# A causal mask inside the scan, a convolution summed in PSUM, and value transposes through the dense products' banks: a hybrid decoder block on one core

## The chip, the core and the metric

The kernel runs on one core of one Trainium2 chip. A core has TensorE (PE in the profile, with its weight loads as PEld), VectorE (DVE), ScalarE (ACT), GpSimd (POOL), and SyncE (SP), which here issues most transfers. Matmuls write to the eight banks of PSUM; DVE and ACT read and write those banks and the on-chip memory SBUF; POOL in this kernel works on SBUF alone.

The metric is the device time in microseconds of one execution. One more execution was recorded by the hardware profiler, and what is said about engines comes from that one.

## The reference

One layer on 1024 tokens with 16 learned tokens in front (1040 positions) and 1024 features. Two branches read the same normalised input: a gated short convolution and stick-breaking attention with 16 heads of 64.

```python
h = xn @ w_in
b_c, c_c, h_c, q, k, v, g_conv, g_attn = jnp.split(h, list(splits), axis=-1)
y_conv = b_c * causal_dwconv(c_c * h_c, conv_w_mix)
branch_conv = y_conv @ w_proj_conv
...
z = jnp.einsum("bqhd,bkhd->bhqk", qb, kb, ...) * scale
causal = s_idx < t_idx
log_beta = jax.nn.log_sigmoid(z)
log_fail = jnp.where(causal, log_beta - z, 0.0)
survive = lax.cumsum(log_fail, axis=3, reverse=True) - log_fail
a = jnp.where(causal, jnp.exp(log_beta + survive), 0.0)
o = jnp.einsum("bhqk,bkhd->bqhd", a, vb)
...
merged = gate_conv * branch_conv + gate_attn * branch_attn
return merged @ w_out
```

The weight of key s for query t is sigmoid(z) times the product, over the keys between s and t, of sigmoid(-z). Keys at or after t have weight 0, and their factor in the product is 1. The convolution has width 3 along positions, one set of three weights for each channel. A gated MLP with a second such convolution follows. All inputs are float32.

## The kernel before, in words

**Exact products from rounded parts.** Every operand of a large product is split into a rounded part and a remainder (`split`, lines 63 to 65: a cast on ACT, a subtraction on DVE or POOL), and a product takes three matmuls: hi x hi, hi x lo, lo x hi (lines 124 to 126).

**The dense products.** `Dense` walks a list of items. An item is 128 output features: 128 columns of a weight matrix, three chunks of about 342 positions, eight steps of three matmuls for a chunk. Before an item starts, the next item's weights are split: ACT writes `whi` (line 64), then POOL writes `wlo` (line 65). A chunk's result is taken from its bank by the item's `evac`. The banks come from `ps_mm`, three of them in turn. `dense.defer(n, fn)` runs `fn` when n further steps have been written.

**Attention.** It works by pairs of heads (8 pairs), and a head in 3 groups of 3 blocks of 114 queries. `stage1` computes for each block the scores z in up to three pieces (lines 325, 326; two banks, `ps_z`), and ACT makes `fl` = sigmoid(-z) and `be` = sigmoid(z). Then `weights`, one step late, does the following: DVE sets the factors on and above the diagonal to 1 by a maximum with the constant `ones_up` over the last 114 columns (line 335), then runs a product scan from the right over all nk columns (line 336, `fl` both as the factor and as the second operand of a minimum); POOL multiplies the scan into `be` (line 338) and zeroes the upper triangle (line 339). The nine widths nk are 128, 242, ... 1040. `stage2` transposes `be` on TensorE into two banks in turn (`ps_tp`, line 372), ACT and DVE split it to `ah` and `al`, and TensorE multiplies with the values (lines 362, 363). A third transpose needs the bank of the first, so it waits until DVE has written that `al`.

**Order.** The program is written as one stream. The loop after line 480 takes steps of `stage1` and `stage2` in turn, by a table of costs, and spends on every step a share of dense steps, so that a pair's own 21 or so dense chunks are done when its attention is done. Each engine executes its own instructions strictly in the order in which the build has placed them. The items of a pair are: three for the convolution (c, h, b), a gate, then value, query and key of the next pair.

**The three places that change.** The convolution: after the third chunk of item h, `conv3` makes `yy` of all 1026 positions at once, a scaled copy on ACT (line 196) and two multiply-adds on DVE (lines 197, 198). The values: `item_v` collects `vt`, and in the three following steps `tokens` transposes it, nine blocks of 128 positions, into the same two `ps_tp` banks (line 257), with a split to `vv` on ACT and DVE. The end of a group: ACT copies one half of `av` to `otmp`, and DVE adds the other half into `ot` (lines 389, 390).

## Time and profile before

| | us |
|---|---|
| three timed runs | 2075.9, 2072.39, 2073.58 |
| median | 2073.58 |
| profiled execution | 2082.49 |
| its span, first to last instruction | 2080.6 |

The median is the time to compare with. Sums made from the profile refer to 2082.49 us and its span; the profiled execution is 8.9 us above the median.

The page gives each engine's busy time, groups of equal instructions, and waits. A matmul's record overlaps the next one's, so TensorE's rate is read from the distance between starts, or from a count in a stretch. In a timeline row the columns are the start in us from the span's start, the duration in us, the engine, the line, the operation with output and inputs, the shapes, and in brackets the idle time before it and what ended it. In the table by stretches the last three columns are the granted clock of TensorE, the busy share of the DMA engines and GB/s.

The span falls into a start (to about 60 us), the attention stage with its dense products (60 to about 1060), the rest of the mixer (to about 1400) and the MLP.

### The profile page before, as it was taken

How to read it: one execution, taken by the hardware profiler on the slowest of the kernel's cores; microseconds unless marked ns; L12 is line 12 of the kernel's file. 1: busy time of each engine (PE TensorE's matmuls, PEld its weight loads, DVE VectorE, ACT ScalarE, POOL GpSimd, SP SyncE). 2: the span in 40 equal slices, each digit the busy share in tenths (PEclk: the TensorE clock that was granted, in tenths of full speed). 3: DMA queues.
4: the chain of work that ended last, by engine and by line, in shares of the span. 5: the costliest groups of instructions: out<-in, count | busy, mean ns of one | idle time of the engine just before them, and what ended most of it. 6: DMA issues, size and time to landing. Idle time of an engine off the chain costs nothing.

```text
span 2080.6 us, 30846 instructions
## 1 busy us (share of the span) xinstructions
PE 1990.9 (96%) x12228; PEld 1861.3 (89%) x12228; DVE 1076.3 (52%) x1689; ACT 851.0 (41%) x1771; POOL 900.2 (43%) x764
## 2 busy tenths in 40 slices
PE   5999999999999999999999989979999999999997
PEld 4999998998999999999999989978898899878886
DVE  6455565655556565654342114785444444445546
ACT  4444454545445454544441213354334434412122
POOL 4343443434344434434212551225655555555353
PEclk9999999999999999999999999989999999999999
DMA  3111101111111101111375674313222122253323
GB/s 134 41 51 41 61 32 51 42 41 52 41 51 42 61 31 52 41 41 61 124 241 173 170 197 132 104 52 102 77 86 82 62 101 66 77 182 102 101 81 132
DMA packets 56029, 177.57 MB, mean 85 GB/s; under 512 B 12728, under 2 KB 12728, under 8 KB 55884
## 3 DMA queue, kind: packets, MB, share of 16 engines
q1 hardware_dynamic: 52560, 165.09, 24.5%
q10 hardware_dynamic: 3324, 10.50, 1.6%
q8 instruction: 96, 1.57, 0.3%
q14 instruction: 49, 0.40, 0.1%
HBM read 131.36 MB, written 44.21 MB: 84 GB/s over the span
## 4 chain that ended last, share of the span: by engine, by line
PE 80%; DVE 9%; ACT 3%; DMA 3%; POOL 2%; issue 2%; DVEq 0%; ACTq 0%; SPq 0%; POOLq 0%
PE mm L124 13%; PE mm L125 12%; PE mm L126 12%; PE st L861 6%; PE st L865 6%; PE st L863 6%; PE st L1155 3%; PE st L1153 3%; PE st L1154 3%; PE tp L372 3%; PE av L362 2%; PE av L363 2%; PE z L326 2%; PE z L325 2%; DVE fl L336 2%
## 5 line engine op out<-in xcount | busy, mean ns | idle before, releaser
L124 PE MATMUL mm<-xnT,whi 128*128 128x342 f32 (+2 forms) x1536 | 506.6, 330 | 3.6 <-ACT xnT L64 3.6
L125 PE MATMUL mm<-xnT,whi 128*128 128x342 f32 (+2 forms) x1536 | 495.4, 323 | 0.5 <-DVE xnT L65 0.5
L126 PE MATMUL mm<-xnT,wlo 128*128 128x342 f32 (+2 forms) x1536 | 492.2, 320 | 0.0
L338 POOL TENSOR_TENSOR be<-be,fl 114x127 f32<-114x127 f32 (+2 forms) x144 | 177.1, 1230 | 412.0 <-DVE fl L336 187.0
L124 PEld LDWEIGHTS mm<-xnT,whi 128*128 128x128 f32 x1536 | 291.0, 190 | 8.4 <-ACT xnT L64 4.1
L125 PEld LDWEIGHTS mm<-xnT,whi 128*128 128x128 f32 x1536 | 291.7, 190 | 2.2 <-DVE xnT L65 1.0
L126 PEld LDWEIGHTS mm<-xnT,wlo 128*128 128x128 f32 x1536 | 290.9, 189 | 0.0
L65 POOL TENSOR_TENSOR wlo<-raw,whi 128x1024 fp32r<-128x1024 f32 x80 | 201.6, 2520 | 187.2 <-ACT whi L64 175.6
L65 POOL TENSOR_TENSOR a_op<-raw,a_op 128x512 fp32r<-128x512 f32 (+1 forms) x136 | 192.2, 1426 | 89.4 <-ACT a_op L64 86.7
L336 DVE TENSOR_TENSOR_SCAN fl<-fl 114x128 f32<-114x128 f32 (+2 forms) x144 | 209.0, 1451 | 4.9
L65 DVE TENSOR_TENSOR al<-tp,ah 128x342 fp32r<-128x342 f32 (+4 forms) x288 | 127.0, 450 | 139.7 <-ACT ah L64 137.6
L64 ACT CAST ah<-tp 128x342 fp32r<-128x342 f32 (+4 forms) x288 | 113.1, 398 | 194.2 <-PE tp L372 185.8
L861 PE MATMUL st<-opT,a_op 128*128 128x258 f32 (+2 forms) x528 | 171.9, 325 | 4.7 <-ACT snap L876 1.7
L863 PE MATMUL st<-opT,a_op 128*128 128x258 f32 (+2 forms) x528 | 169.8, 322 | 2.9 <-DVE opT L65 2.0
L865 PE MATMUL st<-opT,a_op 128*128 128x258 f32 (+2 forms) x528 | 169.3, 321 | 0.0
L327 ACT ACTIVATE fl<-z 114x348 f32<-114x348 f32 (+10 forms) x240 | 111.5, 465 | 131.9 <-PE z L326 124.5
L64 ACT CAST a_op<-raw 128x512 fp32r<-128x512 f32 (+1 forms) x136 | 85.0, 634 | 156.2 <-DMA raw<-in_w_up_gate_dram 51.2
L372 PE MATMUL tp<-ident,be 114*128 114x114 f32 x720 | 119.7, 263 | 29.5 <-DVE al L65 25.1
L1160 DVE TENSOR_TENSOR acc<-acc,st 128x512 f32<-128x512 f32 x144 | 98.5, 687 | 91.2 <-PE st L1155 91.2
L372 PEld LDWEIGHTS tp<-ident,be 114*128 114x128 f32 x720 | 89.0, 138 | 44.6 <-DVE al L65 34.3
L863 PE MATMUL st<-opB,a_op 128*128 128x512 f32 (+2 forms) x396 | 127.4, 322 | 0.0
L861 PE MATMUL st<-opB,a_op 128*128 128x512 f32 (+2 forms) x396 | 127.3, 321 | 0.0
(172 smaller groups left out, 4408.8 us busy)
## 6 DMA issues: line engine op xcount, KB each, us to landing
raw<-in_w_in_dram SPq DMA_DIRECT2D x64, 512.0 KB
raw<-in_w_up_gate_dram SPq DMA_DIRECT2D x44, 512.0 KB
act_d<-owork SPq DMA_DIRECT2D x22, 512.0 KB
araw<-act_d SPq DMA_DIRECT2D x22, 512.0 KB
raw<-in_w_down_dram SPq DMA_DIRECT2D x22, 512.0 KB
y_d<-yy SPq DMA_DIRECT2D x8, 513.0 KB
ga_d<-gt SPq DMA_DIRECT2D x8, 513.0 KB
o_d<-ot SPq DMA_DIRECT2D x8, 513.0 KB
```

The lines of the kernel that those rows point to most:

```text
L64: nc.scalar.copy(hi, src)
L65: (lo_engine or nc.vector).tensor_tensor(lo, src, hi.bitcast(F32), op=ALU.subtract)
L124: nc.tensor.matmul(ps, wh, xh, start=(kb == 0), stop=False)
L125: nc.tensor.matmul(ps, wh, xl, start=False, stop=False)
L126: nc.tensor.matmul(ps, wl, xh, start=False, stop=(kb == KB - 1))
L327: nc.scalar.activation(fl[:, c0:c0 + n], z, AF.Sigmoid, scale=-0.125)
L336: nc.vector.tensor_tensor_scan(fl[:, :nk][:, ::-1], fl[:, :nk][:, ::-1], fl[:, :nk][:, ::-1], 1.0, op0=ALU.mult, op1=ALU.min)
L338: nc.gpsimd.tensor_tensor(be[:, 0:nk - 1], be[:, 0:nk - 1], fl[:, 1:nk], op=ALU.mult)
L372: nc.tensor.transpose(tp[:n, QB * j:QB * (j + 1)], blocks[j][0][:, kb * P:kb * P + n], ident[:QB, :QB])
L861: nc.tensor.matmul(ps, wt[:, 0, k], xh, start=start and kb == 0, stop=False, skip_group_check=True)
L863: nc.tensor.matmul(ps, wt[:, 0, k], xl, start=False, stop=False, skip_group_check=True)
L865: nc.tensor.matmul(ps, wt[:, 1, k], xh, start=False, stop=stop and kb == 3, skip_group_check=True)
```

## The change

- **Mask.** `ones_up` (114 x 114) becomes `upper` (114 x 1040), zero but for the last 114 columns, which hold the triangle of ones. The maximum on DVE ahead of the scan is gone. The scan multiplies as before, and its second operation is now a maximum with `upper` instead of a minimum with `fl`: 1 on and above the diagonal, at least 0 elsewhere.
- **Convolution.** It is done after each chunk of item h instead of after the third, 342 positions at a time. The scaled copy goes to a bank of `ps_mm` (`yacc`), the first multiply-add works in that bank, the second writes `yy` in SBUF. Two DVE instructions of 1026 become six of 342; one on ACT becomes three.
- **Values.** The transposes go to banks of `ps_mm` (`vtp`), and at steps 4, 12 and 20 after the value item instead of 1, 2 and 3. `ps_tp` is left to the attention weights.
- **End of a group.** ACT copies into `ot` itself; `otmp` is gone.
- **Constants.** The table of channel constants is loaded in two parts: 40 columns at the start, 66 later, behind `early`. The start-up pool has two buffers for each tag instead of four.

```diff
-    par = const.tile([P, 106], F32, name="par")
+    par = const.tile([P, 40], F32, name="par")
...
-    ones_up = xnt_pool.tile([QB, QB], F32, name="ones_up")
-    nc.gpsimd.memset(ones_up, 0.0)
-    nc.gpsimd.affine_select(out=ones_up, in_=ones_up, pattern=[[-1, QB]], compare_op=ALU.is_gt,
-                            fill=1.0, base=0, channel_multiplier=1)
+    upper = xnt_pool.tile([QB, NT], F32, name="upper")
+    nc.gpsimd.memset(upper, 0.0)
+    nc.gpsimd.affine_select(out=upper[:, NT - QB:], in_=upper[:, NT - QB:], pattern=[[-1, QB]],
+                            compare_op=ALU.is_gt, fill=1.0, base=0, channel_multiplier=1)
...
-                tp = ps_tp.tile([P, 512], F32, name="tp", tag="tp")
+                tp = ps_mm.tile([P, 512], F32, name="vtp", tag="mm")
...
-            dense.defer(1, lambda: tokens(0, 4, P))
-            dense.defer(2, lambda: tokens(4, 4, P))
-            dense.defer(3, lambda: tokens(8, 1, 16))
+            dense.defer(4, lambda: tokens(0, 4, P))
+            dense.defer(12, lambda: tokens(4, 4, P))
+            dense.defer(20, lambda: tokens(8, 1, 16))
...
             nc.vector.tensor_tensor(c, c, ps, op=ALU.mult)
-            if ci == 2:
+            if ci == 0:
                 st["y"] = work.tile([P, NT], F32, name="yy", tag="wk", bufs=4)
-                conv3(st["y"][:, :NQ], st["c"], NQ, lambda k: w_mix(k, cb))
+            j = ci * CH
+            y, src = st["y"][:, j:j + CH], st["c"][:, j:]
+            acc = ps_mm.tile([P, 512], F32, name="yacc", tag="mm")[:, :CH]
+            nc.scalar.activation(acc, src[:, 2:2 + CH], AF.Copy, scale=w_mix(2, cb))
+            nc.vector.scalar_tensor_tensor(acc, src[:, 1:1 + CH], w_mix(1, cb), acc,
+                                           op0=ALU.mult, op1=ALU.add)
+            nc.vector.scalar_tensor_tensor(y, src[:, 0:CH], w_mix(0, cb), acc,
+                                           op0=ALU.mult, op1=ALU.add)
...
-                nc.vector.tensor_tensor(fl[:, nk - QB:nk], fl[:, nk - QB:nk], ones_up, op=ALU.max)
                 nc.vector.tensor_tensor_scan(fl[:, :nk][:, ::-1], fl[:, :nk][:, ::-1],
-                                             fl[:, :nk][:, ::-1], 1.0, op0=ALU.mult, op1=ALU.min)
+                                             upper[:, NT - nk:][:, ::-1], 1.0,
+                                             op0=ALU.mult, op1=ALU.max)
...
-        tmp = work.tile([P, CH], F32, name="otmp", tag="otmp")
         a, b = (0, 64) if h == 0 else (64, 0)
-        nc.scalar.copy(tmp[a:a + 64], av[b:b + 64])
-        nc.vector.tensor_tensor(ot[a:a + 64, CH * g:CH * (g + 1)], av[a:a + 64], tmp[a:a + 64],
-                                op=ALU.add)
+        o = ot[a:a + 64, CH * g:CH * (g + 1)]
+        nc.scalar.copy(o, av[b:b + 64])
+        nc.vector.tensor_tensor(o, av[a:a + 64], o, op=ALU.add)
...
+    par_ffn = early.tile([P, 66], F32, name="par_ffn")
+    nc.sync.dma_start(par_ffn, channels[:, 40:])
```

The build places each engine's instructions anew. Two places on DVE are shown, first before and then changed. `cc` is the convolution's input, `fl` the factors of the scan, `al` the split of the transposed weights, for which TensorE waits.

DVE at the third chunk of item h, before: the chunk's product, both multiply-adds with a split between them, the splits, and later the mask and scan of 698 columns.

```order
L276 TENSOR_TENSOR cc<-cc,mm 128x342
L197 SCALAR_TENSOR_TENSOR yy<-cc,par,yy 128x1026
L65 TENSOR_TENSOR al<-tp,ah 128x342
L198 SCALAR_TENSOR_TENSOR yy<-cc,par,yy 128x1026
L65 TENSOR_TENSOR al<-tp,ah 128x228
L65 TENSOR_TENSOR al<-tp,ah 100x114
L283 TENSOR_TENSOR yy<-yy,mm 128x342
L335 TENSOR_TENSOR fl<-fl,ones_up 114x114
L336 SCALAR_TENSOR_TENSOR fl<-fl 114x698
```

DVE at the same place, changed (the listing names the scan like a multiply-add; it is the row that writes `fl`):

```order
L343 SCALAR_TENSOR_TENSOR fl<-fl,upper 114x584
L277 TENSOR_TENSOR cc<-cc,mm 128x342
L284 SCALAR_TENSOR_TENSOR yacc<-cc,par,yacc 128x342
L343 SCALAR_TENSOR_TENSOR fl<-fl,upper 114x698
L286 SCALAR_TENSOR_TENSOR yy<-cc,par,yacc 128x342
L65 TENSOR_TENSOR al<-tp,ah 128x228
L65 TENSOR_TENSOR al<-tp,ah 100x114
```

The scan of 698 columns has moved from behind the two splits to ahead of them, between the chunk's two multiply-adds.

ACT at the same place, changed: the cast of the next weights and then the scaled copy.

```order
L336 ACTIVATE be<-z 114x350
L64 CAST whi<-raw 128x1024
L283 ACTIVATE yacc<-cc,par 128x342
L335 ACTIVATE fl<-z 114x348
L336 ACTIVATE be<-z 114x348
```

The scaled copy stands behind the cast of the weights, as the copy of 1026 did.

DVE where the values are split, before:

```order
L65 TENSOR_TENSOR vv<-tp,vv 128x8x64
L335 TENSOR_TENSOR fl<-fl,ones_up 114x114
L336 SCALAR_TENSOR_TENSOR fl<-fl 114x584
L65 TENSOR_TENSOR vv<-tp,vv 128x8x64
L65 TENSOR_TENSOR vv<-tp,vv 16x2x64
L335 TENSOR_TENSOR fl<-fl,ones_up 114x114
L336 SCALAR_TENSOR_TENSOR fl<-fl 114x698
L65 TENSOR_TENSOR al<-tp,ah 128x342
```

And changed:

```order
L343 SCALAR_TENSOR_TENSOR fl<-fl,upper 114x470
L343 SCALAR_TENSOR_TENSOR fl<-fl,upper 114x584
L65 TENSOR_TENSOR vv<-vtp,vv 128x8x64
L343 SCALAR_TENSOR_TENSOR fl<-fl,upper 114x698
L65 TENSOR_TENSOR al<-tp,ah 128x342
```

One split of values instead of three stands ahead of the weights' split; the other two follow later, among the query's.

More of the change, by code (lines that the diff above doesn't have):

```diff
@@ L192, in w_ffn @@
     def w_ffn(k, b):
-        return par[:, 40 + k * NFF + b:40 + k * NFF + b + 1]
+        return par_ffn[:, k * NFF + b:k * NFF + b + 1]
     def conv3(dst, src, n, wt):
@@ L429, in block_kernel @@
     with ExitStack() as p0:
-        small = p0.enter_context(pool("p0s", 4, "right"))
+        small = p0.enter_context(pool("p0s", 2, "right"))
         gb = work.tile([P, NT], F32, name="gb", tag="wk", bufs=4)[:, :D]
         junk = work.tile([P, NT], F32, name="junk", tag="wk", bufs=4)[:, :D]
-        warm = small.tile([P, 1], F32, name="warm", bufs=1)
+        warm = small.tile([P, 1], F32, name="warm", tag="v")
         nc.vector.memset(warm, 1.0)
@@ L470, in block_kernel @@
         dense.load(1)
-        nc.sync.dma_start(par, channels)
+        nc.sync.dma_start(par, channels[:, :40])
         start_items(x_block)
```

## The prediction

> **What bounds the kernel.** I read the table by stretches first: the two halves of the attention stage (60 to 1060 us, where nearly every edited line works) and a stretch of dense products alone. Each row gives PE, PEld, DVE, ACT, POOL busy with counts, then granted clock, DMA share, GB/s.
>
> ```profile
> 110.00:600.00 490.00, 472.94 (x3062) 454.43 (x3061) 285.04 (x440) 237.36 (x545) 200.07 (x224) 0.99 0.14 47
> 600.00:1060.00 460.00, 447.89 (x2915) 432.60 (x2915) 248.81 (x395) 227.46 (x518) 182.62 (x193) 1.00 0.20 64
> 1060.00:1150.00 90.00, 90.00 (x577) 90.00 (x576) 25.77 (x46) 18.78 (x34) 19.21 (x8) 1.00 0.61 195
> ```
>
> TensorE bounds it: 577 matmuls in 90 us are 0.156 us each at full rate, and in the attention stage TensorE lacks only 17.1 + 12.1 = 29 us of work in 950. DVE, which the change relieves, is little over half busy there, so DVE time is worth something only where TensorE waits for it. The waits of PE say where (us, times, longest):
>
> ```profile
> PE tp L372 <- DVE al L65: 25.1, 20, 2.6
> PE tp L372 <- DVE vv L65: 4.4, 6, 0.7
> ```
>
> So 29.5 us, all transposes of weights held by a DVE split. That is the ceiling of the direct gain. The timeline shows them at four kinds of place; in each I ask what the changed order puts ahead of the split.
>
> **Place 1: the mixer convolution, once in each of 8 pairs.** Start, duration, instruction; brackets give the idle time before.
>
> ```profile
> 329.93 1.38 DVE L336 TENSOR_TENSOR_SCAN fl<-fl 114x584 f32<-114x584 f32 x1
> 331.30 0.51 DVE L276 TENSOR_TENSOR cc<-cc,mm 128x342 f32<-128x342 f32 x1
> 333.28 3.21 DVE L197 SCALAR_TENSOR_TENSOR yy<-cc,par,yy 128x1026 f32<-128x1026 f32 x1 [1.47 <-ACT yy L196]
> 336.41 0.50 DVE L65 TENSOR_TENSOR al<-tp,ah 128x342 fp32r<-128x342 f32 x1
> 331.14 1.06 ACT L64 CAST whi<-raw 128x1024 fp32r<-128x1024 f32 x1
> 332.09 1.15 ACT L196 ACTIVATE yy<-cc,par 128x1026 f32<-128x1026 f32 x1
> 331.45 1.23 POOL L338 TENSOR_TENSOR be<-be,fl 114x583 f32<-114x583 f32 x1 [1.38 <-DVE fl L336]
> 333.01 2.39 POOL L65 TENSOR_TENSOR wlo<-raw,whi 128x1024 fp32r<-128x1024 f32 x1
> 336.96 0.30 PE L372 MATMUL tp<-ident,be 114*100 114x114 f32 x1 [1.57 <-DVE al L65]
> L283 DVE TENSOR_TENSOR yy<-yy,mm x24: 478/490/512, 111.1 to 935.0; 128x342 f32<-128x342 f32 x24
> ```
>
> L197 reads two SBUF operands. It starts 0.27 us behind POOL's `wlo` and ends 1.09 us after it (336.49 against 335.40): DVE stood until POOL had finished. L283 has one operand in PSUM, and its 24 calls spread only from 478 to 512 ns. So the new additions, with the running sum in PSUM, should not be held: I take 0.45 us for one (a third of 1.27 us, the free width-1026 call, is 0.42; L283 has 0.49), and 0.5 us for the ACT product (bounds 0.38, a third of L196, and 1.15).
>
> The Trainium skill (SBUF — State Buffer, "Who interferes with whom") states just that: an instruction of DVE with two SBUF inputs and one of GpSimd that reads SBUF exclude each other whole, and one SBUF input leaves DVE free. Trace and rule agree at L197 and L283, and the rule also speaks against the change: the new scan still has two SBUF inputs.
>
> That is where the stall goes. In the new order the 698-wide scan comes third, between the two additions of the last chunk, ahead of the splits. When does it start? The ACT product stands behind the weight cast (ends 332.20), so 332.2 + 0.5 + 0.45 plus handshakes is 333.2; and 0.4 us of transposes now stand ahead of the chunk's last matmul, which moves the cast too: 333.6. `wlo` follows the 584-wide scan (end 331.31) by 1.70 us, and that scan moves by under 0.1: 333.1. POOL wins by 0.5 us. The scan then runs from about 335.2 (as L197 did) for 1.65, the second addition to 337.35, the split of 228 to 337.7. PE resumes at 337.7, not 336.96, with 0.4 us more work behind it (two weight-value products, a transpose and a score product more, a dense matmul less). Net **+0.3 us** a pair, times 8 = **+2.4**. If the scan wins instead, the split ends at 336.0: -1.35 a pair, -10.8. Upper bound: a further 0.7 us for slow PSUM additions, +8.
>
> **Place 2: values, 6 pairs.** The nine value transposes held the two `tp` banks, and the splits `vv` stood in DVE's queue.
>
> ```profile
> 388.50 1.15 DVE L335 TENSOR_TENSOR fl<-fl,ones_up 114x114 f32<-114x114 f32 x1
> 389.69 1.38 DVE L336 TENSOR_TENSOR_SCAN fl<-fl 114x584 f32<-114x584 f32 x1
> 392.59 1.65 DVE L336 TENSOR_TENSOR_SCAN fl<-fl 114x698 f32<-114x698 f32 x1
> 394.16 0.78 DVE L65 TENSOR_TENSOR al<-tp,ah 128x342 fp32r<-128x342 f32 x2
> 387.13 2.39 POOL L65 TENSOR_TENSOR wlo<-raw,whi 128x1024 fp32r<-128x1024 f32 x1
> 391.21 1.22 POOL L338 TENSOR_TENSOR be<-be,fl 114x583 f32<-114x583 f32 x1 [1.69 <-DVE fl L336]
> 391.70 0.51 PE L372 MATMUL tp<-ident,be 114*128 114x114 f32 x3 [0.74 <-DVE vv L65]
> 394.70 0.30 PE L372 MATMUL tp<-ident,be 114*100 114x114 f32 x1 [0.86 <-DVE al L65]
> ```
>
> The first idle time (0.74) goes: the values have other banks. The second is a chain. Without its mask the 584-wide scan waits for the same `wlo` (to 389.52) and ends at 390.7, not 391.06. One `vv` split still stands behind it (0.55, to 391.25), so POOL's `be` product, 0.15 us after the scan's end as before (391.06 to 391.21), is first again and holds the 698-wide scan until about 392.0. Scan to 393.6, split to 394.0, PE resumes at 394.05. That is 0.65 earlier, but five of the nine value transposes (0.1 us each, the last short: 0.45) are still to do: **-0.2** a pair, **-1.2**. Bounds: both idle times gone, -1.6 a pair, -10; above, 0.4 us at the first key chunk, which now waits for a query chunk emptied eight steps earlier, +3.
>
> **Place 3: the longest scan against `wlo`.** The same contest, lost and won:
>
> ```profile
> 352.06 0.37 DVE L335 TENSOR_TENSOR fl<-fl,ones_up 114x114 f32<-114x114 f32 x1 [1.62 <-ACT fl L327]
> 352.46 4.40 DVE L336 TENSOR_TENSOR_SCAN fl<-fl 114x1040 f32<-114x1040 f32 x1
> 352.27 2.41 POOL L65 TENSOR_TENSOR wlo<-raw,whi 128x1024 fp32r<-128x1024 f32 x1
> 357.32 0.52 PE L372 MATMUL tp<-ident,be 114*128 114x114 f32 x3 [1.95 <-DVE al L65]
> 589.90 2.33 DVE L336 TENSOR_TENSOR_SCAN fl<-fl 114x1040 f32<-114x1040 f32 x1
> 589.98 4.43 POOL L65 TENSOR_TENSOR wlo<-raw,whi 128x1024 fp32r<-128x1024 f32 x1
> 472.01 4.39 DVE fl L336
> ```
>
> At 352 POOL was 0.19 us ahead and the scan took 4.40; at 590 DVE was 0.08 ahead and `wlo` took 4.43, which cost PE nothing. Without the mask the scan starts where the mask did, 0.3 to 0.4 us earlier, and wins. The loss occurs in two pairs (the last row, from the chain of waits, is the other): 2 x 2.1 = **-4.2** (bounds -4.2 and 0).
>
> **Place 4: the last pair.**
>
> ```profile
> 972.48 1.38 DVE L336 TENSOR_TENSOR_SCAN fl<-fl 114x584 f32<-114x584 f32 x1
> 974.06 2.62 DVE L336 TENSOR_TENSOR_SCAN fl<-fl 114x698 f32<-114x698 f32 x1
> 974.00 1.22 POOL L338 TENSOR_TENSOR be<-be,fl 114x583 f32<-114x583 f32 x1 [1.69 <-ACT ah L64]
> 977.14 0.43 PE L372 MATMUL tp<-ident,be 114*100 114x114 f32 x1 [2.58 <-DVE al L65]
> ```
>
> Here no `vv` stands between the scans; without the mask the second follows at once and beats `be`. The first starts 0.3 earlier, the second ends at 975.1 and not 976.7: **-1.6**.
>
> **The clock.** A wait costs more than its length where it empties a slot of 3.41 us:
>
> ```profile
> 335.28:338.69 3.41, 1.83 (x12) 1.47 (x12) 3.41 (x6) 0.26 (x1) 0.23 (x2) 1.00 0.46 154
> 338.69:342.11 3.42, 3.42 (x14) 3.38 (x14) 2.52 (x4) 1.35 (x3) 1.12 (x1) 0.50 0.00 0
> 219.22:222.63 3.41, 1.82 (x12) 1.29 (x10) 3.41 (x5) 0.26 (x1) 0.47 (x2) 1.00 0.48 154
> 222.63:226.04 3.41, 3.41 (x23) 3.38 (x23) 2.76 (x5) 1.64 (x4) 0.87 (x1) 1.00 0.02 5
> 458.16:461.57 3.41, 3.41 (x13) 3.37 (x14) 2.61 (x4) 1.35 (x3) 1.02 (x1) 0.50 0.00 0
> 976.98:980.40 3.42, 3.26 (x13) 3.26 (x14) 0.69 (x3) 0.26 (x1) 1.68 (x3) 0.50 0.00 0
> ```
>
> After 1.83 us of PE in a slot the next had clock 0.50 and 14 matmuls, not 23; after 1.82 it did not. So about 1.6 us idle in one slot is the edge, and a half-speed slot costs 1.7 us. Slots at 338.7, 458.2 and 977.0 are such. The last goes with place 4: **-1.7**. At place 1 PE now stands about 0.3 us longer, 1.87 and not 1.57, past the edge. The share of positions that leave 1.58 us of it in one slot is (3.41 - 1.87 + 2 x 0.29)/3.41, 0.62; for 1.57 the same reckoning gives 0.54, and 2 of 8 were seen. I take 4 of 8: **+3.4** (bounds -3.4 and +10).
>
> The Trainium skill (TensorE: Matmul & The Clock Gate, "Why this matters for your kernels") warns of idle gaps over about 3 us. By that page alone none of these stops would open a slot, and the two clock terms would be zero: 2069.0, inside the forecast's own range below. The trace has a half-speed slot behind a stop of 1.57 us, and decides.
>
> **Costed at nothing.** `upper` adds under 1 us of POOL memset at the start, where POOL is mostly idle ahead of its first product; uncovered, +0.8. The smaller start-up pool changes no order on PE before the first value transposes. `ot` takes the copy that `otmp` took, the same two instructions. The table's second part is one more SP issue, between the last two writes of `mm_d` and with no wait of its own; uncovered, +0.4. The convolution sums use dense banks, but each is freed about 3 us after its chunk, and the next matmul that needs it comes 8 steps (24 dense matmuls, 3.7 us, and the attention between them) later.
>
> **Sum**, against the profiled execution of 2082.49 us (span 2080.6; the timed runs have median 2073.58, so I carry the difference over): 2.4 - 1.2 - 4.2 - 1.6 - 1.7 + 3.4 = -2.9, or 2070.7.
>
> **Rivals.** (a) *The stalls go as drawn* (chance 0.25). It needs DVE to reach the exclusive reading ahead of POOL at place 1; I have it late by 0.5 us, and an ACT product or a `wlo` off by that much turns it. Then -10.8 at place 1, its two slots -3.4, and the terms of places 2 to 4 with the third slot (-8.7): -23, **2051**. For it speaks place 3, where 0.3 us decides; against it, that the cast stands ahead of the ACT product in all pairs. (b) *The longer single stops empty clock slots* (0.2). One mechanism: places 1 and 2 now each have one stop of 1.7 to 2.0 us, and if 12 of these 14 open a slot, 8 more than I took, that is +13.6, **2084**. It turns slower from about 6 slots. For it: from 338.69 to 458.16, one pair, are 35.0 slots, so a bad position can stay bad. Against it: place 2 was two short waits and never opened one. (c) *The new bank sharing stops PE* at value and key chunks: 0.4 us, 7 times, +2.8, **2073.5**; inside the forecast's range, and I give it no separate chance.
>
> **How the numbers follow.** Forecast 0.55, own range 2064 to 2076; (a) 0.25; (b) 0.2. A measurement here can tell about 0.2%, 4.1 us. The forecast's range falls below 2069.4 in four cases of ten and above 2077.7 in hardly one: faster 0.25 + 0.22 = 0.47, slower 0.2 + 0.04 = 0.24, same 0.29. The 8-in-10 range reaches into (a) and (b): 2048 to 2082.
>
> **What would show it.** Right: scans of 698 over 3 us at place 1 and PE waits of 2 us there; additions near 0.45 us with no spread; no scan of 1040 over 2.4 us; one wait at place 2. Wrong: `wlo` over 4 us beside the 698-wide scan, which is (a); more than six half-speed slots, which is (b); PE waiting at L124 or L258, which is (c).

## The result and the profile after

The changed kernel takes 2096.22 us (median of 4 runs, 2092.74 to 2099.2), the kernel before 2074.74 us in 4 runs beside it. The ratio is 1.0099, with a 95% interval of 1.0077 to 1.012: slower by 1.0%. The forecast was 2070.7 us, with a range of 2048 to 2082 us. The profiled execution took 2099.2 us, its span 2097.4 us. One execution further down, of the kernel with the convolution alone, ran at a granted clock of 0.752 and took 2423.85 us; no ratio or median counts it.

The table by stretches of the changed kernel, the two halves of the attention stage, the stretch of dense products, and last the whole stage from the first score product to the last weight-value product:

```profile
110.00:600.00 490.00, 469.78 (x3027) 454.58 (x3025) 269.84 (x376) 236.54 (x547) 199.60 (x222) 0.99 0.14 47
600.00:1060.00 460.00, 441.66 (x2865) 427.55 (x2866) 236.21 (x339) 222.43 (x511) 178.68 (x194) 0.99 0.17 57
1060.00:1150.00 90.00, 90.00 (x576) 90.00 (x575) 29.89 (x54) 26.92 (x52) 19.23 (x8) 1.00 0.68 209
77.10:1033.90 956.80, 917.02 (x5928) 886.94 (x5927) 518.99 (x724) 469.74 (x1084) 394.64 (x438) 0.99 0.14 47
```

The same stage before:

```profile
74.50:1018.60 944.10, 913.32 (x5929) 878.75 (x5928) 543.70 (x836) 466.39 (x1068) 394.10 (x438) 0.99 0.14 47
```

DVE has 25 us less to do, as the change intends, and the stage is 12.7 us longer. TensorE has the same 5928 matmuls; its idle time went from 30.8 to 39.8 us (+9.0), and its busy time rose by 3.7 us. There are three more half-speed slots (shown below), which at the 1.7 us of the prediction would be 5.1; where the other 1.4 us went, I did not trace. The span grew by 16.8 us; the other 4.1 lie ahead of the first score product (74.5, now 77.1) and behind the stage. That start lay anywhere from 72.5 to 76.6 us in the experiments below (without the execution at 0.752), whatever their edit, and I put nothing down to it.

What TensorE waits for (us, times, longest):

```profile
PE tp L380 <- DVE al L65: 22.8, 14, 1.8
PE av L371 <- DVE al L65: 15.0, 7, 2.2
```

These 37.8 us replace the 29.5 of before. The timeline puts them at the same kinds of place.

**The convolution, 7 pairs.** Start, duration, instruction; idle time in brackets:

```profile
336.76 0.58 DVE L284 SCALAR_TENSOR_TENSOR yacc<-cc,par,yacc 128x342 f32<-128x342 f32 x1 [0.86 <-ACT yacc L283]
337.24 3.38 DVE L343 TENSOR_TENSOR_SCAN fl<-fl,upper 114x698 f32<-114x698 f32 x1
340.55 0.54 DVE L286 SCALAR_TENSOR_TENSOR yy<-cc,par,yacc 128x342 f32<-128x342 f32 x1
336.75 2.40 POOL L65 TENSOR_TENSOR wlo<-raw,whi 128x1024 fp32r<-128x1024 f32 x1
341.45 0.37 PE L371 MATMUL av<-al,vv 128*128 128x228 f32 x1 [2.12 <-DVE al L65]
L284 DVE SCALAR_TENSOR_TENSOR yacc<-cc,par,yacc x24: 553/578/580, 100.4 to 934.3; 128x342 f32<-128x342 f32 x24
```

The scan reaches the exclusive reading (of SBUF, which a DVE instruction with two SBUF operands and a reading POOL instruction get only one at a time) 0.49 us behind `wlo` (337.24 against 336.75) and takes 3.38 us. The additions in PSUM spread from 553 to 580 ns only (last row, its durations are minimum, median, maximum): they are not held, though `wlo` runs beside them.

**The longest scan, 7 pairs.** This place was to become free. The product at L346 belongs to the 926-wide block ahead:

```profile
353.69 1.82 POOL L346 TENSOR_TENSOR be<-be,fl 114x925 f32<-114x925 f32 x1 [2.09 <-DVE fl L343]
355.59 0.28 POOL L347 TENSOR_SCALAR_AFFINE_SELECT be<-be 114x114 f32<-114x114 f32 x1
355.84 2.39 POOL L65 TENSOR_TENSOR wlo<-raw,whi 128x1024 fp32r<-128x1024 f32 x1
355.45 0.46 ACT L335 ACTIVATE fl<-z 114x344 f32<-114x344 f32 x1
356.01 4.40 DVE L343 TENSOR_TENSOR_SCAN fl<-fl,upper 114x1040 f32<-114x1040 f32 x1 [1.64 <-ACT fl L335]
360.87 0.51 PE L380 MATMUL tp<-ident,be 114*128 114x114 f32 x3 [1.54 <-DVE al L65]
```

The scan starts 0.10 us after its last sigmoid (355.91), as early as it can; `wlo` has started 0.17 us before. This happens in all 7 pairs after the first; before, it happened in 2.

**Values and the last pair.** One wait a pair at the values, and a short one at the end. The first row is the first score product of the 584-wide block, to count from:

```profile
268.37 0.30 PE L333 MATMUL z<-kk,qh 128*114 128x292 f32 x1
274.53 1.22 POOL L346 TENSOR_TENSOR be<-be,fl 114x583 f32<-114x583 f32 x1 [1.38 <-DVE fl L343]
274.89 2.32 DVE L343 TENSOR_TENSOR_SCAN fl<-fl,upper 114x698 f32<-114x698 f32 x1
277.68 0.31 PE L380 MATMUL tp<-ident,be 114*100 114x114 f32 x1 [1.78 <-DVE al L65]
993.70 0.30 PE L380 MATMUL tp<-ident,be 114*100 114x114 f32 x1 [0.99 <-DVE al L65]
```

**The clock.** A slot with a convolution stop and the slot behind it:

```profile
338.71:342.12 3.41, 1.29 (x9) 1.05 (x8) 2.86 (x4) 0.00 (x0) 1.80 (x2) 1.00 0.44 154
342.12:345.54 3.42, 3.42 (x15) 3.42 (x14) 1.01 (x2) 1.08 (x3) 0.47 (x3) 0.50 0.00 0
```

Such half-speed slots begin at 222.7, 342.1, 461.6, 581.1, 820.0 and 939.5 us: 6 in the stage, all behind convolution stops, where before had 3.

### The profile page after: what moved, and what is told of

It is laid out like the page before. It is cut to its first block, busy times and chain, and to the rows that moved or that the text cites. A ratio compares the mean times of both kernels' runs of the same rounds, so it can differ in the third digit from the quotient of the medians.

```text
span 2097.4 us, 30756 instructions
## 1 busy us (share of the span) xinstructions
PE 1996.5 (95%) x12228; PEld 1872.0 (89%) x12228; DVE 1048.6 (50%) x1577; ACT 855.1 (41%) x1787; POOL 901.7 (43%) x764
## 3 DMA queue, kind: packets, MB, share of 16 engines
q8 instruction: 96, 1.57, 0.3%
## 4 chain that ended last, share of the span: by engine, by line
PE 77%; DVE 11%; ACT 4%; DMA 3%; POOL 3%; issue 2%; ACTq 0%; DVEq 0%; POOLq 0%; SPq 0%
PE mm L124 13%; PE mm L125 12%; PE mm L126 12%; PE st L870 5%; PE st L874 5%; PE st L872 5%; DVE fl L343 4%; PE st L1164 3%; PE st L1162 3%; PE st L1163 3%; PE tp L380 3%; PE av L370 2%; PE av L371 2%; POOL a_op L65 2%; PE z L334 2%
## 5 line engine op out<-in xcount | busy, mean ns | idle before, releaser
L346 POOL TENSOR_TENSOR be<-be,fl 114x127 f32<-114x127 f32 (+2 forms) x144 | 177.5, 1233 | 404.3 <-DVE fl L343 332.7
L343 DVE TENSOR_TENSOR_SCAN fl<-fl,upper 114x128 f32<-114x128 f32 (+2 forms) x144 | 247.6, 1721 | 137.2 <-ACT fl L335 124.5
L65 POOL TENSOR_TENSOR wlo<-raw,whi 128x1024 fp32r<-128x1024 f32 x80 | 191.4, 2393 | 202.2 <-ACT whi L64 202.2
L870 PE MATMUL st<-opB,a_op 128*128 128x512 f32 (+2 forms) x396 | 127.6, 322 | 0.0
L872 PE MATMUL st<-opB,a_op 128*128 128x512 f32 (+2 forms) x396 | 127.5, 322 | 0.0
L874 PE MATMUL st<-opB,a_op 128*128 128x512 f32 (+2 forms) x396 | 127.1, 321 | 0.0
```

The costliest lines, as they stand in the source:

```text
L65: (lo_engine or nc.vector).tensor_tensor(lo, src, hi.bitcast(F32), op=ALU.subtract)
L343: nc.vector.tensor_tensor_scan(fl[:, :nk][:, ::-1], fl[:, :nk][:, ::-1], upper[:, NT - nk:][:, ::-1], 1.0, op0=ALU.mult, op1=ALU.max)
L346: nc.gpsimd.tensor_tensor(be[:, 0:nk - 1], be[:, 0:nk - 1], fl[:, 1:nk], op=ALU.mult)
L870: nc.tensor.matmul(ps, wt[:, 0, k], xh, start=start and kb == 0, stop=False, skip_group_check=True)
L872: nc.tensor.matmul(ps, wt[:, 0, k], xl, start=False, stop=False, skip_group_check=True)
L874: nc.tensor.matmul(ps, wt[:, 1, k], xh, start=False, stop=stop and kb == 3, skip_group_check=True)
```

## The experiments

Two theories were tested first. **A**: every stop is a DVE instruction with two SBUF operands that comes to the exclusive reading just behind POOL, and the change altered who comes first. **B**: TensorE's own order or the shared PSUM banks made the new stops. The experiments ran later, in three groups on three chips; the kernel before, timed beside each group, has medians of 2065.37, 2065.84 and 2065.51 us. All ratios are to the kernel before timed beside it, with 95% intervals; they are not quotients of the medians, which come out up to 0.15% higher. The changed kernel itself was not timed again, so it is compared with the experiments by ratio and by the length of the stage, not by median. The stage is measured from the first score product to the last weight-value product of the profiled execution.

| kernel | median us | ratio | stage us | half-speed slots in it |
|---|---|---|---|---|
| before (result above) | 2074.74 | 1 | 944.1 | 3 |
| changed (result above) | 2096.22 | 1.0099 (1.0077 to 1.012) | 956.8 | 6 |
| fold alone | 2067.18 | 1.0000 (0.9983 to 1.0016) | 940.0 | 1 |
| convolution alone | 2083.98 | 1.0091 (1.0070 to 1.0112) | 955.6 | 7 |
| values alone | 2074.37 | 1.0033 (1.0011 to 1.0055) | 945.1 | 3 |
| changed, mask undone | 2089.28 | 1.0105 (1.0084 to 1.0127) | 958.6 | 7 |
| changed, convolution undone | 2078.06 | 1.0050 (1.0028 to 1.0072) | 950.0 | 4 |
| changed, values undone | 2079.1 | 1.0051 (1.0025 to 1.0076) | 950.5 | 5 |
| changed, pause on POOL | 2079.76 | 1.0065 (1.0044 to 1.0086) | 950.4 | 10 |
| changed, `wlo` in 4 pieces | 2041.09 | 0.9880 (0.9860 to 0.9900) | 914.1 | 0 |
| changed, `wlo` in 8 pieces | 2043.05 | 0.9881 (0.9850 to 0.9911) | 913.3 | 0 |
| fold alone, 4 pieces | 2042.76 | 0.9887 (0.9869 to 0.9906) | 915.9 | 1 |
| before, 4 pieces | 2053.85 | 0.9931 (0.9906 to 0.9957) | 926.8 | 1 |

For the convolution alone, stage and slots are those of its second profile, described below. The stops in the expectations are counted some 0.15 us longer than the idle times given here (1.72 for 1.55 us at the longest scan).

### Undoing the mask

```diff
...
+                nc.vector.tensor_tensor(fl[:, nk - QB:nk], fl[:, nk - QB:nk], ones_up, op=ALU.max)
                 nc.vector.tensor_tensor_scan(fl[:, :nk][:, ::-1], fl[:, :nk][:, ::-1],
-                                             upper[:, NT - nk:][:, ::-1], 1.0,
-                                             op0=ALU.mult, op1=ALU.max)
+                                             fl[:, :nk][:, ::-1], 1.0, op0=ALU.mult, op1=ALU.min)
```

> The changed kernel with the two-step mask put back (the 114x114 maximum, then the scan with the minimum); convolution and values stay changed. Theory A (order at GpSimd): the fold moved the 926-wide scan, its product on GpSimd and so the next low-part subtraction `wlo` forward by 0.35 us, and took away the short operation with which DVE came first, so `wlo` now beats the 1040-wide scan in every pair. With the mask back that scan takes 4.4 us in 2 or 3 pairs and not 7, 5 stops of 1.72 us go (-8.6), and the convolution's stop grows by the mask of the 698-wide scan (0.3 us x 8, +2.4): about 2090 us (2086 to 2096). Rival B (TensorE's own order or the shared PSUM banks made the new stops): all 7 stops stay and the mask costs its own time, 2098 us or more.

Measured 1.0105, without the gain that A expected: the long scans take 4.4 us in all 7 later pairs even with the mask. That all 7 stops stay is what B expected; the next experiment, where they come although TensorE's order is that of the kernel before, speaks against B's cause. The mask shows the exclusive reading at its barest, at the convolution of this kernel:

```profile
217.68 2.35 DVE L342 TENSOR_TENSOR fl<-fl,ones_up 114x114 f32<-114x114 f32 x1
220.44 0.56 DVE L65 TENSOR_TENSOR al<-tp,ah 128x228 fp32r<-128x228 f32 x2
220.92 1.60 DVE L343 TENSOR_TENSOR_SCAN fl<-fl 114x698 f32<-114x698 f32 x1
217.51 2.39 POOL L65 TENSOR_TENSOR wlo<-raw,whi 128x1024 fp32r<-128x1024 f32 x1
```

An operation of 114x114 that takes 0.28 us elsewhere takes 2.35 here and ends just behind `wlo` (220.03 against 219.90). The splits then come before the scan, and the stop is 1.1 us, not 2.1.

### The fold alone

The changed kernel with convolution and values as before; TensorE's order is row for row that of the kernel before.

```diff
-                tp = ps_mm.tile([P, 512], F32, name="vtp", tag="mm")
+                tp = ps_tp.tile([P, 512], F32, name="tp", tag="tp")
...
-            dense.defer(4, lambda: tokens(0, 4, P))
+            dense.defer(1, lambda: tokens(0, 4, P))
...
-            if ci == 0:
+            if ci == 2:
                 st["y"] = work.tile([P, NT], F32, name="yy", tag="wk", bufs=4)
...
-            acc = ps_mm.tile([P, 512], F32, name="yacc", tag="mm")[:, :CH]
...
+                conv3(st["y"][:, :NQ], st["c"], NQ, lambda k: w_mix(k, cb))
...
```

> The changed kernel with convolution and values as before; of the change only the folded mask (and the copy into `ot`, the split table) is left. TensorE's order is that of the kernel before. Theory A: the 1040-wide scan loses to `wlo` in 6 to 8 pairs (+8 us against before), the convolution's stop is 0.35 us shorter (-2.8), the last pair gains 1.6: 2078 us (2073 to 2082). Rival B: the fold alone does what was forecast, the two long scans of 4.4 us vanish: 2067 us or less, no scan of 1040 over 2.4 us.

Measured 1.0000, and A's stops: the long scan took 4.3 to 4.4 us in all 7 later pairs, though of the change only the mask, the copy into `ot` and the split table are left. Theory B is refuted by this. A's 2078 us was reckoned from the base of the result above, where it is a ratio of 1.0016 (its range 0.9992 to 1.0035); the measurement lies inside that range. At the stops, the convolution's fell from 1.6 us of idle time to 1.0 to 1.3, the values' two from 0.73 and 0.86 to 0.4 and 0.5, the last pair's from 2.6 to 1.0 (A had named the first and the last of these), and no half-speed slot stands behind any stop after the first pair.

```profile
75.10:1015.10 940.00, 910.91 (x5928) 877.02 (x5928) 504.17 (x692) 467.38 (x1068) 407.86 (x438) 1.00 0.13 47
391.28 0.51 PE L373 MATMUL tp<-ident,be 114*128 114x114 f32 x3 [0.40 <-DVE vv L65]
393.93 0.31 PE L373 MATMUL tp<-ident,be 114*100 114x114 f32 x1 [0.49 <-DVE al L65]
```

### The convolution alone

The kernel before with the new `evac_h` and nothing else of the change.

```diff
-            if ci == 2:
+            if ci == 0:
                 st["y"] = work.tile([P, NT], F32, name="yy", tag="wk", bufs=4)
-                conv3(st["y"][:, :NQ], st["c"], NQ, lambda k: w_mix(k, cb))
...
+            acc = ps_mm.tile([P, 512], F32, name="yacc", tag="mm")[:, :CH]
...
```

> The kernel before with the convolution alone changed (per chunk, summed in PSUM). Theory A: the 698-wide scan takes the place of the long addition behind `wlo`, with its mask ahead of it: a stop of 2.3 to 2.6 us in place of 1.75 (+6), 1040-wide scans lose in 2 or 3 pairs as before, and 6 half-speed slots stand behind the stops and not 3 (+5): 2086 us (2081 to 2092). Rival C (the fold alone costs the time): 2075 us, stops of 1.75 us or less.

Measured 1.0091: nearly the whole loss, in one part. As a ratio, theory A's 2086 us is 1.005 (1.003 to 1.008), so the measurement lies above A's range, though not by more than its own interval. The profiled execution was the one at a granted clock of 0.752, nearly from end to end, and its stops can't be compared with the others'. The same kernel was traced once more (2085.98 us):

> The convolution-only kernel once more, for a profile of an execution at the usual clock (the first one's profile stood at a granted clock of 0.752 throughout). Theory A2 (a tie between the 1040-wide scan's mask and GpSimd's masking step, broken by hundredths of a microsecond): with the convolution changed, the last sigmoid of the 1040-wide block ends 0.0 to 0.1 us behind the end of the 926-wide product and not 0.06 before it, so `wlo` wins in all 7 later pairs and that scan takes 4.4 us (a stop of 2.1 us each); the convolution's own stop is 1.3 us (the mask of the 698-wide scan waits for `wlo`), the values' two are as before. Rival D: the 1.0% of this kernel is the convolution's own stop, 2.3 us or more, and half-speed slots behind it; long scans as before.

It came out as A2 said, and not as A, which had long scans lose in 2 or 3 pairs. The stop at the convolution is short (1.1 us of idle time, the mask waits there as in the kernel with the mask undone), and the long scan loses in 7 of 7:

```profile
350.37 1.82 POOL L345 TENSOR_TENSOR be<-be,fl 114x925 f32<-114x925 f32 x1 [2.09 <-DVE fl L343]
352.26 0.28 POOL L346 TENSOR_SCALAR_AFFINE_SELECT be<-be 114x114 f32<-114x114 f32 x1
352.51 2.41 POOL L65 TENSOR_TENSOR wlo<-raw,whi 128x1024 fp32r<-128x1024 f32 x1
351.74 0.46 ACT L334 ACTIVATE fl<-z 114x344 f32<-114x344 f32 x1
352.70 4.39 DVE L343 TENSOR_TENSOR_SCAN fl<-fl 114x1040 f32<-114x1040 f32 x1
357.56 0.51 PE L379 MATMUL tp<-ident,be 114*128 114x114 f32 x3 [1.96 <-DVE al L65]
```

The contest is a tie. Take the end of the last sigmoid of the 1040-wide block minus the end of the 926-wide product on POOL. Here it is 0.00 to 0.07 us in the 7 pairs, and the scan loses all. With the values alone it is -0.05 to -0.13 in six, and the scan wins; -0.01 in the one that it loses. Before, it is -0.05 to -0.13 where it wins and 0.00 and 0.05 where it loses. In the changed kernel with the mask undone it is 0.01 to 0.07, and the scan loses all. A pair that wins, before:

```profile
587.72 1.83 POOL L338 TENSOR_TENSOR be<-be,fl 114x925 f32<-114x925 f32 x1 [2.09 <-DVE fl L336]
589.62 0.39 POOL L339 TENSOR_SCALAR_AFFINE_SELECT be<-be 114x114 f32<-114x114 f32 x1
589.03 0.46 ACT L327 ACTIVATE fl<-z 114x344 f32<-114x344 f32 x1
589.59 0.28 DVE L335 TENSOR_TENSOR fl<-fl,ones_up 114x114 f32<-114x114 f32 x1 [1.62 <-POOL be L338]
```

The sigmoid ends at 589.49, the product at 589.55; the mask operation starts at 589.59 and POOL's masking step is held by it, 0.39 us and not 0.28, so the scan (589.90) comes 0.08 us ahead of `wlo` (589.98). With the fold the same difference is 0.33 to 0.49 us in every later pair, since the whole chain ahead of it on DVE and POOL is a mask shorter, and there is no tie any more. Which hundredths the convolution moves, I did not trace further. Six of this kernel's 7 half-speed slots begin at these long-scan stops.

### The values alone

The kernel before with the values' transposes moved.

```diff
-                tp = ps_tp.tile([P, 512], F32, name="tp", tag="tp")
+                tp = ps_mm.tile([P, 512], F32, name="vtp", tag="mm")
...
-            dense.defer(1, lambda: tokens(0, 4, P))
+            dense.defer(4, lambda: tokens(0, 4, P))
...
```

> The kernel before with the values' transposes alone changed (dense banks, issued 4, 12 and 20 steps later). Theory A: one wait in place of two, 0.0 to 0.4 us less a pair, nothing else moves: 2073 us (2069 to 2077). Rival B (shared banks stop TensorE at the dense products or the value transposes): 2077 us or more, with TensorE waiting at the first dense product of a chunk.

Measured 1.0033, above A's forecast and with none of B's waits: two waits became one, but one of 2.5 us instead of 0.74 and 0.86.

```profile
384.73 0.30 PE L325 MATMUL z<-kk,qh 128*114 128x292 f32 x1
394.73 0.30 PE L372 MATMUL tp<-ident,be 114*100 114x114 f32 x1 [2.53 <-DVE al L65]
```

DVE's chain (scan, `be` product on POOL, scan, split) sets the end of the wait at the same point as before: 9.95 to 9.99 us behind the first score product of the 584-wide block (the first row) in all six pairs, where before had 9.96 to 9.98 (there, too, this product stands at 384.73). In that time TensorE does 33 dense matmuls in both kernels, but 9 transposes of values before and 4 here. Moved behind the wait, the other five leave it standing for 0.9 us longer a pair (2.5 against 1.6).

### Undoing convolution or values

The changed kernel with one of the last two diffs turned round.

> The changed kernel with the convolution as before: fold and values are left. Theory A2: stops of 1.40 (convolution), 1.66 (long scan, all pairs) and one of 1.95 us (values) a pair, 5.0 in place of 6.0 us, and few half-speed slots since only the values' stop is long enough: ratio to before 1.003 (1.000 to 1.006). Rival C (the fold costs the time): 1.008 or more.

> The changed kernel with the values as before: fold and convolution are left. Theory A2: stops of 2.30 (convolution), 1.72 (long scan) and 0.57 + 0.65 us (values) a pair, 5.25 in place of 6.0 us, and about 6 half-speed slots behind the convolution's stops: ratio to before 1.007 (1.004 to 1.010), that is, the convolution takes most of the loss. Rival: 1.003 or less, the values' single stop is what costs.

Measured 1.0050 and 1.0051, both inside A2's ranges, though not A2's reading of the second, that the convolution takes most of the loss: each of the two parts is worth about half of it when the rest of the change is there (the stage is 6.8 and 6.3 us shorter than the changed kernel's, of 12.7). Alone they cost 0.9% and 0.3%, so the parts do not add up: with the fold the long scan loses in every pair anyway, and the convolution has less left to spoil. In one place of the first of these kernels TensorE waited 0.41 us at a key chunk's first product for a query chunk; no other wait of theory B's kind over 0.4 us stands in the attention stage of any of these profiles.

### A pause on POOL

Three short memsets behind the masking step of the 926-wide block, over columns that are zero already; the other engines keep their order.

```diff
+                if nk == P + 7 * QB:
+                    for _ in range(3):
+                        nc.gpsimd.memset(be[:, nk - 1:], 0.0)
```

> The changed kernel with three memsets of 114x115 on GpSimd (about 0.2 us each, of columns that are zero already) behind the masking step of the 926-wide block; they read no SBUF, and TensorE, DVE and ACT keep their orders. Theory A: `wlo` then starts 0.6 us later, behind the start of the 1040-wide scan, which takes 2.33 us in all 8 pairs and not 4.4; `wlo` takes 4.4 us and nobody waits for it; the 7 stops of 1.72 us go, so 12 us less than the changed kernel, a ratio to before of about 1.004 (1.001 to 1.007). Rival B (the stops come from TensorE's order, the PSUM banks or late sigmoids): the stops stay and the ratio is 1.010.

```profile
354.00 0.70 POOL L352 MEMSET be<- 114x115 f32 x3
354.91 3.69 POOL L65 TENSOR_TENSOR wlo<-raw,whi 128x1024 fp32r<-128x1024 f32 x1
354.08 2.33 DVE L343 TENSOR_TENSOR_SCAN fl<-fl,upper 114x1040 f32<-114x1040 f32 x1 [1.64 <-ACT fl L335]
```

With more work on POOL the stage is 6.4 us shorter: the scan comes first in all 7 later pairs and takes 2.33 us, `wlo` takes 3.69, and nobody waits for either. All 7 stops there are gone. The ratio is 1.0065, within the range but above the centre, because 10 half-speed slots now stand in the stage: behind 5 of the 7 convolution stops and 5 of the 6 values stops, which had opened none in the changed kernel's profile. So the gain is 6.4 us and not the 12 expected.

### `wlo` in pieces

```diff
-                split(hi, lo, raw, nc.gpsimd)
+                nc.scalar.copy(hi, raw)
+                for c in range(0, D, 256):
+                    nc.gpsimd.tensor_tensor(lo[:, c:c + 256], raw[:, c:c + 256],
+                                            hi[:, c:c + 256].bitcast(F32), op=ALU.subtract)
```

> The changed kernel with `wlo` made in four GpSimd instructions of 256 columns and not one of 1024. Theory A (a DVE instruction with two SBUF operands waits for the whole GpSimd instruction that holds the reading): a scan now waits for one piece of 0.6 to 0.7 us, not for 2.4; the 1040-wide scan ends within 3 us, the stops fall from 2.30 to 0.9 (convolution), 1.72 to 0.4 (long scan) and 1.95 to 1.3 us (values), and no half-speed slot is left in the attention stage: some 22 us and 10 us of slots less, ratio to before 0.995 (0.990 to 1.000). Rival E (GpSimd goes from piece to piece without letting DVE read): the scans still take 4.4 us and the ratio is 1.010.

Measured 0.9880, better than A's whole range (0.990 to 1.000), since the stops shrank further than A said (of idle time, 0.50 us at most at the convolution, 0.27 at the values, none over 0.15 at the longest scan of the later pairs): 2041.09 us, faster than both kernels. At the two places shown above:

```profile
343.18 4.84 POOL L111 TENSOR_TENSOR wlo<-raw,whi 128x256 fp32r<-128x256 f32 x4
343.36 2.73 DVE L346 TENSOR_TENSOR_SCAN fl<-fl,upper 114x1040 f32<-114x1040 f32 x1 [1.64 <-ACT fl L338]
327.31 4.12 POOL L111 TENSOR_TENSOR wlo<-raw,whi 128x256 fp32r<-128x256 f32 x4
327.79 1.72 DVE L346 TENSOR_TENSOR_SCAN fl<-fl,upper 114x698 f32<-114x698 f32 x1
330.33 0.37 PE L374 MATMUL av<-al,vv 128*128 128x228 f32 x1 [0.45 <-DVE al L65]
73.90:988.00 914.10, 907.11 (x5928) 877.58 (x5927) 484.18 (x724) 469.69 (x1084) 450.17 (x609) 1.00 0.14 49
```

The scan still comes 0.18 us late, but now waits for one piece: 2.73 us, not 4.40. The four pieces then take 4.84 us together instead of 2.39, and TensorE waits for none of them in the stage. TensorE's idle time in the stage is 7.0 us instead of 39.8, no half-speed slot is left, and the stage is 42.7 us shorter than the changed kernel's.

> The changed kernel with `wlo` in eight pieces of 128 columns. Theory A: a DVE instruction now waits for 0.4 us at most, the convolution's stop falls from 0.65 to 0.4 us: 2 us less than in four pieces, ratio to before 0.987 (0.985 to 0.990). Rival G (each piece costs GpSimd 0.1 us more and `wlo` comes late for the dense products): TensorE waits for `wlo`, 0.990 or more.

Eight pieces give 0.9881, no better. The convolution's stop did not shrink further (0.60 to 0.64 us of idle time; 0.45 to 0.50 with four pieces), so A missed there, and no wait for `wlo` stands in the stage, so G did too.

> The kernel with the fold alone (convolution and values as before), with `wlo` in four pieces. Theory A: its stops of 1.40 (convolution) and 1.66 us (long scan) a pair fall to about 0.5 and 0.3, the values' 0.57 and 0.65 hardly move: 2.2 us x 8 = 18 us less than the fold alone, ratio to before 0.991 (0.988 to 0.996). Rival E: 1.000 as without the pieces.

> The kernel before with `wlo` in four pieces. Theory A (the exclusive reading is what every stop hangs on, and the change only moves it about): 1.75 us at the convolution falls to about 0.7, the long scans of 4.4 us are gone, of the values' 0.88 and 1.01 some 0.5 are left; 2.4 us x 7 = 17 us, with the slots 20: ratio to before 0.990 (0.986 to 0.994), so within 0.3% of the changed kernel in pieces. Rival F (without the contention the change itself is worth the 10 us that its shorter DVE work suggests): 0.993 or more here, against 0.988 for the changed kernel in pieces.

Measured 0.9887 and 0.9931. The first is inside A's range. The second is inside A's range (0.986 to 0.994) and at the edge of rival F's; what decides for F is that A wanted it within 0.3% of the changed kernel in pieces, and that the values' stops did not fall to A's 0.5 us. The kernel before in pieces keeps them and the last pair's,

```profile
383.71 1.14 DVE L338 TENSOR_TENSOR fl<-fl,ones_up 114x114 f32<-114x114 f32 x1
387.00 0.30 PE L375 MATMUL tp<-ident,be 114*100 114x114 f32 x1 [1.20 <-DVE al L65]
```

where the mask waits behind the 583-wide product on POOL and pushes scan and split back. So with `wlo` out of the way the change is worth 0.5 to 0.6% (0.9880 against 0.9931; 12.8 us in the medians, taken on two chips, and 12.7 in the stage), and the fold alone gives nearly all of it. The sign of the change depends on what GpSimd does beside it.

## Why the prediction was wrong

By its own steps, with TensorE's idle time at each place, summed over all pairs that have a stop there, from the timelines:

| step | forecast us | measured us |
|---|---|---|
| place 1, convolution | +2.4 | +2.6 (12.4 to 15.0) |
| place 2, values | -1.2 | +1.3 (9.5 to 10.9) |
| place 3, longest scan | -4.2 | +7.1 (3.8 to 10.9) |
| place 4, last pair | -1.6 | -1.6 (2.6 to 1.0) |
| clock | -1.7 + 3.4 | +3.7 (busy time of the stage) |
| short stops in the first pair | none | -1.1 |

The measured rows add up to 12.0 of the 12.7 us in the stage, against -2.9 forecast. Of the miss of 25.5 us in the median (2096.22 against 2070.7), place 3 makes 11.3, place 2 makes 2.5 and the clock 2.0; 4.1 lie ahead of and behind the stage, and 5.9 come from the base (the profiled execution was 8.9 us above the median before, and 3.0 after). The small rest cancels.

**Place 3 failed, and it decides.** The step read: "Without the mask the scan starts where the mask did, 0.3 to 0.4 us earlier, and wins." The first half is right, the conclusion is not. The 926-wide scan ahead of it lost its mask too, so its product, the masking step and `wlo` moved forward by the same 0.4 us, while the last sigmoid, which TensorE paces, did not. I moved one runner of a race and left the other standing, although `wlo` starts from a chain that begins with a scan of the same kind. And I read the mask as a cost ahead of the scan; in the pairs that won before it was the operation that came to the reading first. The pause (stops gone) and the fold alone (stops in all pairs) show it. The convolution alone loses the same pairs by the tie, so undoing one of the two parts doesn't bring them back.

**Place 1 was right in mechanism, and its total partly by luck**: POOL first by 0.49 us where 0.5 was forecast, the scan at 3.38 us, stops of 2.1 us. But a stop grew by 0.56 us a pair (1.58 to 2.14), not by 0.3, in 7 pairs; the sum agrees because the first pair's stop of 1.28 us, which was to grow like the others, went. The additions took 0.54 to 0.58 us and not 0.45, but without spread. The Trainium skill (SBUF — State Buffer, "Who interferes with whom") says that the order of issue, not the shape of the operation, decides who blocks; the tie above and the mask of 2.35 us agree, and with pieces the wait is one piece long.

**Place 2 was wrong by 0.4 us a pair, in one term.** The wait's end came 0.66 us earlier as forecast (0.65): 9.31 us behind the first score product of the 584-wide block (277.68 against 268.37) and not 9.97 (394.70 against 384.73). The five transposes moved behind it were put at 0.45 us; they take 0.9 (values alone: 2.5 us of idle time against 1.6, with the wait's end unmoved). So a pair gains 0.66, loses 0.9, and stands 0.2 us longer.

**The clock.** 4 convolution stops of 8 were to open a slot; 6 of 7 did, and the slot of the last pair went as forecast. Rival (b) named about 6 slots as the point from which the change turns slower, but priced 12 at these two places; 6 came, the values opened none in this profile, and without place 3 they would not have reached 2096. Rival (c) did not occur: TensorE waited at no value transpose for more than 0.2 us.

**The base.** The sum was made against an execution 8.9 us above the median of the runs then known, and I carried that difference over while booking as gains the two lost scans and the half-speed slots which that execution had. A typical execution may have had fewer of them. Beside the experiments the kernel before ranged from 2061.3 to 2090.8 us: most executions lie under 2074, at a granted clock of 0.991 to 0.994, and seven above it, at 0.992 falling to 0.987. A tie that falls now one way and now the other would look like this, but no execution under 2074 us was traced, so this stays open. Part of the 9 us between this base and 2074.74 lies behind the stage and not in the change: in the profiles of the result, before and changed alike, DVE waits 22.0 and 26.3 us for transfers of `gal`, and TensorE once 4.8 us for DVE there, beside a half-speed stretch of 6.8 us; of the experiments' profiles only that with eight pieces has a wait of TensorE of 2 us or more there (2.5).

**What held.** The work costed at nothing (the larger constant, `ot`, the split table, the banks) shows in no wait.

## What to carry to other kernels

When an edit shortens work on one side of a contest for an exclusive resource, redo the start of both sides from their common ancestor, and treat a margin under 0.1 us as a coin that every later edit tosses again. Shorten the instruction that holds the resource before polishing those that wait for it: cutting GpSimd's 2.4 us subtraction into four made both kernels faster, and turned a change of +1.0% into one of -0.5%. Work of the bounding engine that happens to stand in front of a wait is cover; moving it behind the wait costs its length.

## What the runs showed of the hardware

**Waiting is for the whole instruction.** With two SBUF operands a DVE operation of 0.28 us took 2.35 us behind a POOL subtraction of 2.39, and POOL's subtraction took 3.69 to 4.84 us behind or between scans. Between two POOL pieces of 0.7 us DVE got the reading at once (scan 2.73 us, 2.33 when free). POOL's memsets, which read nothing, held no scan.

**The clock goes by slots on a fixed grid.** Half-speed slots of 3.413 us, or whole multiples, lie at whole multiples of that length from one another. I took the idle time of TensorE in each full-speed slot that lies wholly in the stage, where it was 1.2 us or more, in the eleven profiles that have a half-speed slot there. Of 58 slots with under 1.57 us none was followed by half speed, of 36 with 1.57 to 1.83 us 12 were, and of 36 with 1.88 us or more all were. The Trainium skill (TensorE: Matmul & The Clock Gate, "What's actually happening") describes a free-running window of 3413 ns, which agrees; its half speed after an idle window does not, since here some 1.8 us, about half a window, are enough, and the longest stop at these places in the changed kernel is 2.16 us.

**A bad position repeats.** In the changed kernel the convolution's stops end at 221.62, 341.45, 461.23, 581.11 and 700.95 us, 119.8 us apart and so 35.1 slots. Against the grid a stop moves by some 0.35 us a pair, and half-speed slots follow four times (222.7, 342.1, 461.6, 581.1) before the fifth stop falls across two slots, with 1.70 us of idle time in the first of them, and opens none. The pair behind it lasts 118.3 us.
